# GpSimd's elementwise work moved to VectorE and ScalarE in five stages of a hybrid decoder layer

## The chip, the cores and the metric

The kernel runs on one core of a Trainium2 chip. The metric is the time of one execution on the device in microseconds. The core has TensorE (matrix products; in the profile PE, and PEld for its weight loads), VectorE (DVE), ScalarE (ACT), GpSimd (POOL) and SyncE (SP), each with a queue of its own that is worked off in order, and 16 DMA engines. Engines wait for each other by semaphores.

## The reference

One decoder layer on x of 1024 tokens by 1024 channels, in float32:

```python
h = rmsnorm(x, norm_mix)
pa, pb, pc, pg = split(h @ w_in)
ya = u * (tril(w_s) @ layernorm(v) + b_s)        # u, v = gelu(pa); chunks of 128 tokens
yb = softmax(q k^T / 8 + c_i - c_j, causal) @ v  # 8 heads of 64; c = cumsum(log_sigmoid(f))
yc = rwkv7(token_shift(pc))                      # 8 heads of 64, state per token:
     # S = S * d - (S kk) (kk a)^T + v k^T ;  y = S r ; groupnorm, bonus, gate
merged = g0 * (ya @ p_a) + g1 * (yb @ p_b) + g2 * (yc @ p_c)   # g = sigmoid(pg + bias)
x = x + merged @ w_out
x = x + (silu(gt) * up) @ w_down                 # gt, up = split(rmsnorm(x) @ w_gate_up)
return rmsnorm(x, norm_final)
```

## The kernel before

Large products are made of three matmuls each: both operands are split into a high part, cast by ScalarE to the type that TensorE takes, and a low part, the rest: `hi*hi + hi*lo + lo*hi` (L156 to L158, tiles `w_hi`, `w_lo`, `o_hi`, `o_lo`, `T_hi`, `T_lo`). The low part is one subtraction of two inputs, and who makes it is what the change is about.

The program goes through these stages, with the times of the profiled execution:

- **Head, 0 to 85 us.** x arrives in pieces, is normalised in two halves of 512 tokens (sums of squares at L470 and L473, scaling at L482 to L484), turned by TensorE (L492) and split into `h_hi` and `h_lo`. Gates are computed by a product of seven half-size products (class `Seven`, Strassen's scheme), which needs sums of blocks of h (`b11` to `b22`, `t2`) and their splits (`T1` to `T4`, `B22`, 40 operations at L335 and L336), and sums of weight blocks (`sums`, L367 to L375, splits `o_hi`, `o_lo`).
- **Gates, 85 to 345.** 14 rounds of `Seven` on `w_in` (tiles `ps_f`).
- **Recurrent branch, 345 to 885** (`rwkv_branch`). Eight units of 512 columns pass through `begin` (decay, keys `kb` and `kr`), `finish` (a triangular solve on VectorE in 31 serial steps of two operations, L1217 and L1219, tiles `tmp` and `X`) and `chain` (the state `S`). Between their steps the generator `projections` issues the other products of h (tiles `ps_g`, `ps_r`), so that TensorE has work.
- **Attention, 885 to 1200** (`attention_branch`). For each head and block of 128 queries: scores `lp` on TensorE, the gate's row `lg = cq - ck` on GpSimd (L1481) with the causal mask (L1482), the sum with row maximum on VectorE (L1485), the exponential on ScalarE (L1488), scaling (L1490), turning (L1495) and a copy to `PT` (L1496). `lg` has three buffers. Projections of v and of yc (`project`) run in between.
- **Merge and output.** 1200 to 1368: the spatial gating (`v` at L700, `ps_m`, `ya_hi`, `ya_lo`) and `project` with p_b and p_a. 1368 to 1480: `w_out` (`ps_o`). Then the second norm, the feed-forward's `Seven` (1520 to 1915) and the last product (`ps_d`), in which VectorE makes the low parts already (L947).

`w_split` (L135 to L140) splits a weight block of up to 128x1056 for all stages; its low part goes to GpSimd:

```python
nc.scalar.copy(hi, raw)
low[0].tensor_tensor(lo, raw, hi.bitcast(F32), ALU.subtract)    # low = [nc.gpsimd]
```

Weights and both parts have two buffers each. The order of instructions in each engine's queue is set by the framework's scheduler when the program is built; it follows the order of the code loosely.

Of the kernel before, what the change touches and what calls it, by code (L numbers as in the profile page):

```python
# [63 lines left out]
def kernel(ctx: ExitStack, tc: tile.TileContext, a: dict, out: bass.AP):  # L64
# [254 lines left out]
    class Seven:  # L319
# [17 lines left out]

        def prepared(self, src):
            o = [self.piece(n, (4, P), F32R) for n in ("o_hi", "o_lo")]
            self.split(o, src, nc.gpsimd)  # L340
            return o
# [14 lines left out]

        def sums(self, f, g, scratch=()):

# [9 lines left out]
            nc.vector.tensor_tensor(s2, s1, A11, ALU.subtract)  # L368
            yield self.prepared(s2)
            nc.vector.tensor_tensor(A21, A11, A21, ALU.subtract)  # L370
            yield self.prepared(A21)
            yield self.prepared(s1)
            yield self.prepared(A22)
            s4 = scratch.pop() if scratch else s2
            nc.vector.tensor_tensor(s4, A12, s2, ALU.subtract)  # L375
            yield self.prepared(s4)

# [73 lines left out]
    def low_rank(half, wts):  # L451
        for n, ci in enumerate((12, 13)):
            ps = gps.tile([P, HALF], F32, name="ps_l", tag="g")
            gemm_t(ps, wts[n], h_hi, h_lo, half)
            carry[n] = shift(ps, ci, half, carry[n], (lw, lg)[n][half])

    fetched = [gs.fetch(0)]
    load_x(1, 0)
    fetched.append(gs.fetch(1))
    load_x(1, 4)  # L460
    b11, b21, b12, b22, t2, t3 = ([None] * 4 for _ in range(6))
    for half in range(2):
        xi = x_in[half]
# [14 lines left out]
        for b in (0, 2, 1, 3):  # L478
            for q in range(4):
# [3 lines left out]
                else:  # L483
                    nc.vector.tensor_scalar(xt, xt, r[:, q:q + 1], None, op0=ALU.mult)  # L484
        if half == 0:

            ops0 = gs.sums(0, fetched[0][0], [h22_tile(i, F32).rearrange("p (a b) -> p a b", a=4) for i in range(5)])
        for k in range(4):
            for kt in (k, 4 + k):
# [5 lines left out]
                if half == 0:  # L495
                    hi, lo = hh(kt, 0)
                    nc.scalar.activation(hi, ps, AF.Copy, scale=pc("norm_mix", kt))
                    nc.vector.scalar_tensor_tensor(lo, ps, pc("norm_mix", kt), hi.bitcast(F32), op0=ALU.mult, op1=ALU.subtract)
                    nc.gpsimd.tensor_tensor(b, hi.bitcast(F32), lo.bitcast(F32), ALU.add)
                else:  # L500
                    nc.scalar.activation(b, ps, AF.Copy, scale=pc("norm_mix", kt))
            if half == 1:
                t2[k] = gs.piece("t2")
                nc.vector.tensor_tensor(b11[k], b12[k], b11[k], ALU.subtract)
                nc.vector.tensor_tensor(t2[k], b22[k], b11[k], ALU.subtract)
                nc.gpsimd.tensor_tensor(b12[k], b22[k], b12[k], ALU.subtract)
                gs.split(T2[k], t2[k], nc.vector)
        if half == 0:
            begun = [gs.begin(0, fetched[0])]
            first = [next(ops0)]  # L510
    begun.append(gs.begin(1, fetched[1]))
    for T, src in ((T3, b12), (T1, b11)):
        for k in range(4):
            gs.split(T[k], src[k], nc.vector)
            if T is T3:
                nc.gpsimd.tensor_tensor(b21[k], b21[k], t2[k], ALU.subtract)
    first += [next(ops0) for _ in range(2)]
# [34 lines left out]
    with ExitStack() as st:  # L552
# [15 lines left out]
        for half in range(2):  # L568
# [4 lines left out]
            for hp in range(4):  # L573
# [7 lines left out]
                for ps, bias, dst in ((ps_w, "c_w0", sg_d), (ps_a, "c_a0", av_d), (ps_g, None, gl_d)):  # L581
# [5 lines left out]
                    nc.sync.dma_start(dst[cs, ts], t)  # L587
    lrst.close()
    rwkv_branch(tc, a, locals())
    lora.close()  # L590


    def y_split(yd, yp, own=False):
        for k in range(4):
# [88 lines left out]
    with ExitStack() as st:  # L683
# [12 lines left out]
        for c in range(8):  # L696
# [6 lines left out]
            for half in range(2):  # L703
# [67 lines left out]
    with ExitStack() as st:  # L771
# [4 lines left out]
        for half in range(2):  # L776
# [5 lines left out]
            for b in range(4):  # L782
# [4 lines left out]
                for i in range(2):  # L787
# [216 lines left out]
def rwkv_branch(tc, a, e):  # L1004
# [4 lines left out]
    with ExitStack() as st:  # L1009
# [67 lines left out]
        def begin(n, u):  # L1077
# [58 lines left out]
        def finish(n, u):  # L1136
# [127 lines left out]
        def chain(n, u):  # L1264
# [133 lines left out]
def attention_branch(tc, a, e):  # L1398
# [6 lines left out]
    with ExitStack() as st:  # L1405
# [39 lines left out]
        for hp in range(4):  # L1445
# [10 lines left out]
            for grp in range(4):  # L1456
# [6 lines left out]
                for qi in range(2):  # L1463
# [68 lines left out]
```

## Time and profile before

| | |
|---|---|
| median of 3 runs | 2143.12 us (2140.16 to 2145.07) |
| profiled execution | 2139.3 us, span 2137.4 us |
| busy TensorE | 2000.8 us (94%), 11773 matmuls |
| busy VectorE, ScalarE, GpSimd | 1260.3, 882.2, 824.2 us |
| mean granted clock of TensorE | 0.967 |

The profile gives the busy time of each engine by stretch, groups of instructions by source line, what each engine waited for, and the instructions in order of time. The granted clock is a share of the full 2.4 GHz; 0.5 is the lower level of 1.2 GHz.

### The profile page before, as it was taken

The page shows a single profiled execution, that of the slowest core. Times are in us where ns is not written, and L with a number is a line of the kernel's source. Part 1 is how long each engine was busy: PE and PEld are TensorE (multiplying, and loading weights), DVE is VectorE, ACT ScalarE, POOL GpSimd, SP SyncE. Part 2 cuts the span into 40 slices and gives each one's busy share as a digit, 9 for nine tenths or more (in the row PEclk, how much of TensorE's full clock was granted, in tenths as well). Part 3 has the DMA queues.
Part 4 walks back from the last instruction along what each step waited for, and adds up shares of the span by engine and source line. Part 5 has one row for each costly group of instructions (what it writes and reads, how often), then busy time and mean ns, then how long its engine had stood idle before and what let it go on. Part 6 is the DMA issues. An engine that isn't in the chain of part 4 may idle for free. (4 is left out here: it accounts for less than half of the span.)

```text
span 2137.4 us, 31459 instructions
## 1 busy us (share of the span) xinstructions
PE 2000.8 (94%) x11773; PEld 1598.6 (75%) x11773; DVE 1260.3 (59%) x2398; ACT 882.2 (41%) x1566; POOL 824.2 (39%) x630
## 2 busy tenths in 40 slices
PE   5899999899889899899999989998999999999998
PEld 4688886676777667777666668897778887878886
DVE  8754454777677764245466594436655444556966
ACT  6433335334454454357554322245323222224435
POOL 5654451223232232233444432344676666530000
PEclk8899999899999999999899999999999999999999
DMA  4233335333233322543343753443232332349433
GB/s 124 84 112 116 116 102 195 108 92 107 83 111 93 94 81 80 171 116 99 104 125 102 274 180 99 129 154 98 79 111 90 115 99 91 107 158 327 135 99 123
DMA packets 254700, 260.91 MB, mean 122 GB/s; under 512 B 21430, under 2 KB 195588, under 8 KB 254548
## 3 DMA queue, kind: packets, MB, share of 16 engines
q1 hardware_dynamic: 218388, 208.53, 31.1%
q10 hardware_dynamic: 32928, 41.16, 6.0%
q0 software_dynamic: 3232, 9.21, 1.6%
q8 instruction: 92, 1.51, 0.3%
q14 instruction: 60, 0.49, 0.1%
HBM read 176.77 MB, written 77.89 MB: 119 GB/s over the span
## 5 line engine op out<-in xcount | busy, mean ns | idle before, releaser
L139 POOL TENSOR_TENSOR w_lo<-w_raw,w_hi 128x1024 fp32r<-128x1024 f32 (+2 forms) x114 | 271.1, 2380 | 438.9 <-ACT w_hi L138 438.6
L156 PE MATMUL ps_f<-T_hi,o_hi 128*128 128x512 f32 x576 | 226.7, 394 | 8.4 <-ACT o_hi L335 5.9
L157 PE MATMUL ps_f<-T_lo,o_hi 128*128 128x512 f32 x576 | 227.2, 394 | 7.4 <-DVE T_lo L336 7.4
L158 PE MATMUL ps_f<-T_hi,o_lo 128*128 128x512 f32 x576 | 226.1, 393 | 0.4 <-POOL o_lo L336 0.4
L336 POOL TENSOR_TENSOR o_lo<-s,o_hi 128x512 fp32r<-128x512 f32 x105 | 150.8, 1436 | 85.1 <-ACT o_hi L335 79.1
L138 ACT CAST w_hi<-w_raw 128x1024 fp32r<-128x1024 f32 (+2 forms) x114 | 112.6, 989 | 138.2 <-PE ps_p L157 30.0
L156 PEld LDWEIGHTS ps_f<-T_hi,o_hi 128*128 128x128 f32 x576 | 109.1, 189 | 34.2 <-ACT o_hi L335 6.3
L157 PEld LDWEIGHTS ps_f<-T_lo,o_hi 128*128 128x128 f32 x576 | 109.2, 190 | 32.5 <-DVE T_lo L336 9.4
L158 PEld LDWEIGHTS ps_f<-T_hi,o_lo 128*128 128x128 f32 x576 | 109.3, 190 | 24.0 <-POOL o_lo L336 0.8
L157 PE MATMUL ps_d<-w_lo,a_hi 128*128 128x512 f32 x272 | 106.7, 392 | 1.7 <-DVE w_lo L947 1.7
L158 PE MATMUL ps_d<-w_hi,a_lo 128*128 128x512 f32 x272 | 106.7, 392 | 0.0
L156 PE MATMUL ps_d<-w_hi,a_hi 128*128 128x512 f32 x272 | 104.7, 392 | 0.0
L335 ACT CAST o_hi<-s 128x512 fp32r<-128x512 f32 x105 | 65.0, 619 | 94.2 <-DVE s L368 45.8
L367 DVE TENSOR_TENSOR s<-up_raw 128x512 f32<-128x512 f32 x35 | 27.9, 797 | 126.1 <-DMA up_raw<-in_w_gate_up_dram 118.2
L336 POOL TENSOR_TENSOR o_lo<-up_raw,o_hi 128x512 fp32r<-128x512 f32 x70 | 90.5, 1293 | 27.0 <-ACT o_hi L335 15.6
L375 DVE TENSOR_TENSOR s<-w_raw,s 128x512 f32<-128x512 f32 x35 | 60.3, 1724 | 59.9 <-POOL o_lo L336 59.9
L1481 POOL TENSOR_SCALAR lg<-ck,cq 128x128 f32<-128x128 f32 (+7 forms) x64 | 50.4, 788 | 100.9 <-PE tp L1495 95.5
L871 ACT CAST a_hi<-a_raw 128x1024 fp32r<-128x1024 f32 (+1 forms) x42 | 41.2, 981 | 110.9 <-PE ps_d L157 92.3
L1217 DVE TENSOR_TENSOR tmp<-N,X 128x60 f32<-128x60 f32 (+24 forms) x248 | 77.1, 311 | 9.3 <-DMA N<-nd 1.5
L156 PE MATMUL ps_g<-h_hi,w_hi 128*128 128x512 f32 x192 | 81.6, 425 | 1.0 <-ACT w_hi L138 1.0
L1485 DVE CUSTOM_DVE_ANT_0 lg<-lp,lg 128x128 f32<-128x128 f32 (+7 forms) x64 | 47.9, 753 | 56.2 <-POOL lg L1482 48.6
L158 PE MATMUL ps_g<-h_hi,w_lo 128*128 128x512 f32 x192 | 76.9, 400 | 2.0 <-POOL w_lo L139 2.0
(485 smaller groups left out, 5760.7 us busy)
## 6 DMA issues: line engine op xcount, KB each, us to landing
w_raw<-in_w_in_dram SPq DMA_DIRECT2D x50, 512.0 KB, 4.2
gt<-gate_d ACTq DMA_DIRECT2D x24, 512.0 KB, 3.4
up_raw<-in_w_gate_up_dram SPq DMA_DIRECT2D x44, 256.0 KB, 3.2
w_raw<-in_w_gate_up_dram SPq DMA_DIRECT2D x22, 512.0 KB, 3.9
a_raw<-act_S SPq DMA_DIRECT2D x20, 512.0 KB, 4.1
w<-in_w_down_dram SPq DMA_DIRECT2D x18, 512.0 KB, 6.3
gate_d<-c SPq DMA_DIRECT2D x33, 256.0 KB, 2.1
w_raw<-in_w_out_dram SPq DMA_DIRECT2D x16, 512.0 KB, 5.7
```

The lines of the kernel that those rows point to most:

```text
L138: nc.scalar.copy(hi, raw)
L139: low[0].tensor_tensor(lo, raw, hi.bitcast(F32), ALU.subtract)
L156: nc.tensor.matmul(ps, lhs[0], rhs[0], start=first, stop=False)
L157: nc.tensor.matmul(ps, lhs[0], rhs[1], start=False, stop=False)
L158: nc.tensor.matmul(ps, lhs[1], rhs[0], start=False, stop=last)
L335: nc.scalar.copy(dst[0], src)
L336: eng.tensor_tensor(dst[1], src, dst[0].bitcast(F32), ALU.subtract)
L375: nc.vector.tensor_tensor(s4, A12, s2, ALU.subtract)
L871: nc.scalar.copy(hi, raw)
L1217: nc.vector.tensor_tensor(tv, N[:, 0:kx, kx].unsqueeze(1).to_broadcast([P, m, kx]), X[:, i0:8, kx:kx + 1].to_broadcast([P, m, kx]), ALU.mult)
L1481: nc.gpsimd.tensor_scalar(lg[:, 0:nk], ck[h][:, 0:nk], -1.0, cq[:, qb, hd:hd + 1], op0=ALU.mult, op1=ALU.add)
L1485: nc.vector.tensor_tensor_reduce(lg[:, 0:nk], lp[:, 0:nk], lg[:, 0:nk], 1.0, NEG, ALU.add, ALU.max, mx)
```

## The change

The elementwise work of GpSimd goes to VectorE in the head (first two weight blocks, five `o_lo`, `b12`, `b21`), in the recurrent branch (`w_lo`, half of `kb`, `x_lo`, `y_lo`), in the attention and the projections (`w_lo`, `y_lo`, `ya_lo`) and in w_out (`w_lo`). In the head the copies `b` of the first half are made by ScalarE from PSUM, deferred by four tiles, and the normalisation of the second half is written ahead of the first gate's products. The gate's rows of the attention go to ScalarE. In the rounds of `Seven` for gates and feed-forward GpSimd keeps its work: `low[0]` is switched over and back.

```diff
-        def prepared(self, src):
+        def prepared(self, src, eng=None):
             o = [self.piece(n, (4, P), F32R) for n in ("o_hi", "o_lo")]
-            self.split(o, src, nc.gpsimd)
+            self.split(o, src, eng or nc.gpsimd)
...
+    low[0] = nc.vector
     fetched = [gs.fetch(0)]
     load_x(1, 0)
     fetched.append(gs.fetch(1))
     load_x(1, 4)
+    low[0] = nc.gpsimd
...
-    for half in range(2):
+    def normed(half):
...
+    def turned(half, xi):
+        plain = []
...
-                    nc.gpsimd.tensor_tensor(b, hi.bitcast(F32), lo.bitcast(F32), ALU.add)
+
+                    plain.append((b, ps, kt))
+                    for b_, ps_, kt_ in [plain.pop(0)] if len(plain) > 4 else []:
+                        nc.scalar.activation(b_, ps_, AF.Copy, scale=pc("norm_mix", kt_))
...
-                nc.gpsimd.tensor_tensor(b12[k], b22[k], b12[k], ALU.subtract)
+                nc.vector.tensor_tensor(b12[k], b22[k], b12[k], ALU.subtract)
...
-        if half == 0:
-            begun = [gs.begin(0, fetched[0])]
-            first = [next(ops0)]
+    xi0, _ = normed(0)
+    turned(0, xi0)
+    xi1, root = normed(1)
+
+    ops0 = gs.sums(0, fetched[0][0], [h22_tile(i, F32).rearrange("p (a b) -> p a b", a=4) for i in range(5)], nc.vector)
+    begun = [gs.begin(0, fetched[0])]
+    first = [next(ops0)]
+    turned(1, xi1)
     begun.append(gs.begin(1, fetched[1]))
...
-                nc.gpsimd.tensor_tensor(b21[k], b21[k], t2[k], ALU.subtract)
+                nc.vector.tensor_tensor(b21[k], b21[k], t2[k], ALU.subtract)
...
     lrst.close()
+    low[0] = nc.vector
     rwkv_branch(tc, a, locals())
...
-            nc.gpsimd.tensor_tensor(lo, raw, hi.bitcast(F32), ALU.subtract)
+            nc.vector.tensor_tensor(lo, raw, hi.bitcast(F32), ALU.subtract)
...
-                nc.gpsimd.tensor_tensor(lo[:, sl], uf, hi[:, sl].bitcast(F32), ALU.subtract)
+                nc.vector.tensor_tensor(lo[:, sl], uf, hi[:, sl].bitcast(F32), ALU.subtract)
...
             if half == 1:
+                low[0] = nc.gpsimd
                 fs = Seven(fx, 25, (B11, B21) + (None,) * 5, w_gu, lambda f: (f * P, DFF + f * P), act_done)
...
-            nc.gpsimd.tensor_tensor(hl[1], sq, hl[0].bitcast(F32), ALU.subtract)
+            nc.vector.tensor_tensor(hl[1], sq, hl[0].bitcast(F32), ALU.subtract)
...
-                nc.gpsimd.tensor_tensor(kb[hs, :, 1 - h, :], v3(av)[hs], v3(pi)[hs], ALU.mult)
+                nc.vector.tensor_tensor(kb[hs, :, 1 - h, :], v3(av)[hs], v3(pi)[hs], ALU.mult)
...
-            nc.gpsimd.tensor_tensor(hl[1], r, hl[0].bitcast(F32), ALU.subtract)
+            nc.vector.tensor_tensor(hl[1], r, hl[0].bitcast(F32), ALU.subtract)
...
-                        nc.gpsimd.tensor_scalar(lg[:, 0:nk], ck[h][:, 0:nk], -1.0, cq[:, qb, hd:hd + 1], op0=ALU.mult, op1=ALU.add)
+                        nc.scalar.activation(lg[:, 0:nk], ck[h][:, 0:nk], AF.Identity, bias=cq[:, qb, hd:hd + 1], scale=-1.0)
```

VectorE at the end of the head, before (`T..` and `h22` are low parts of h's sums, `u` the first round's result):

```order
L336 TENSOR_TENSOR T42_lo_199<-b_335,T42_hi_198 128x512
L336 TENSOR_TENSOR T43_lo_201<-b_353,T43_hi_200 128x512
L336 TENSOR_TENSOR h22_609<-b_480,h22_608 128x512
L336 TENSOR_TENSOR h22_613<-b_500,h22_612 128x512
L336 TENSOR_TENSOR h22_617<-b_520,h22_616 128x512
L336 TENSOR_TENSOR h22_605<-b_460,h22_604 128x512
L382 TENSOR_TENSOR u_357<-u_357,ps_f_626 128x512
```

The same place now (`o_lo` are low parts of the weight sums):

```order
L336 TENSOR_TENSOR o_lo_580<-h22_409,o_hi_579 128x512
L336 TENSOR_TENSOR T40_lo_195<-b_293,T40_hi_194 128x512
L336 TENSOR_TENSOR o_lo_584<-h22_407,o_hi_583 128x512
L336 TENSOR_TENSOR T41_lo_197<-b_309,T41_hi_196 128x512
L336 TENSOR_TENSOR T42_lo_199<-b_326,T42_hi_198 128x512
L336 TENSOR_TENSOR T43_lo_201<-b_344,T43_hi_200 128x512
L336 TENSOR_TENSOR o_lo_596<-h22_408,o_hi_595 128x512
L336 TENSOR_TENSOR h22_613<-b_500,h22_612 128x512
L336 TENSOR_TENSOR o_lo_601<-h22_405,o_hi_600 128x512
L336 TENSOR_TENSOR h22_609<-b_480,h22_608 128x512
L336 TENSOR_TENSOR h22_617<-b_520,h22_616 128x512
L336 TENSOR_TENSOR h22_605<-b_460,h22_604 128x512
```

The four later `o_lo`, which stood in GpSimd's queue, now stand between the splits of VectorE.

VectorE in a triangular solve of the recurrent branch, before:

```order
L1217 TENSOR_TENSOR tmp_3748<-N_3742,X_3747 128x66
L1219 TENSOR_TENSOR X_3747<-X_3747,tmp_3748 128x6x11
L1217 TENSOR_TENSOR tmp_3748<-N_3742,X_3747 128x60
L1219 TENSOR_TENSOR X_3747<-X_3747,tmp_3748 128x6x10
L1217 TENSOR_TENSOR tmp_3748<-N_3742,X_3747 128x54
L1219 TENSOR_TENSOR X_3747<-X_3747,tmp_3748 128x6x9
L1217 TENSOR_TENSOR tmp_3748<-N_3742,X_3747 128x48
```

The same steps now:

```order
L1234 TENSOR_TENSOR tmp_3748<-N_3742,X_3747 128x66
L1236 TENSOR_TENSOR X_3747<-X_3747,tmp_3748 128x6x11
L1234 TENSOR_TENSOR tmp_3748<-N_3742,X_3747 128x60
L1236 TENSOR_TENSOR X_3747<-X_3747,tmp_3748 128x6x10
L139 TENSOR_TENSOR w_lo_3994<-w_raw_3991,w_hi_3993 128x1024
L445 SCALAR_TENSOR_TENSOR gt_3975<-ps_g_3920,omu_140,sh_3976 128x512
L1234 TENSOR_TENSOR tmp_3748<-N_3742,X_3747 128x54
L441 MEMSET sh_4075 128x1
L1236 TENSOR_TENSOR X_3747<-X_3747,tmp_3748 128x6x9
```

A weight split of 128x1024 stands between two steps of the solve; there are 29 of them in the branch. 36 of the 114 `w_lo` stay on GpSimd.

ScalarE in the attention, first group of queries, before (L1488 is the exponential, L1496 the copy of the turned rows):

```order
L1488 ACTIVATE lg_8755,sm_8763<-lg_8755,mx_8760 128x256
L1496 COPY PT_8696<-tp_8730 128x128
L1488 ACTIVATE lg_8787,sm_8795<-lg_8787,mx_8792 128x384
L1496 COPY PT_8695<-tp_8751 128x2x128
L284 ACT_TABLE_LOAD
L284 ACTIVATE gt_8883<-ps_r_8882 128x256
L1496 COPY PT_8696<-tp_8767 128x2x128
L1488 ACT_TABLE_LOAD
L1488 ACTIVATE lg_8804,sm_8812<-lg_8804,mx_8809 128x384
L1496 COPY PT_8779<-tp_8799 128x3x128
```

The same place now (L1505 and L1513 are those two, L1498 the gate's row):

```order
L1505 ACTIVATE lg_8739,sm_8747<-lg_8739,mx_8744 128x256
L1498 ACTIVATE lg_8755<-ck_8451,cq_72 128x256
L1513 COPY PT_8696<-tp_8730 128x128
L1498 ACTIVATE lg_8787<-ck_8449,cq_72 128x384
L1513 COPY PT_8695<-tp_8751 128x2x128
L1498 ACTIVATE lg_8804<-ck_8451,cq_72 128x384
L1505 ACTIVATE lg_8755,sm_8763<-lg_8755,mx_8760 128x256
L1505 ACTIVATE lg_8787,sm_8795<-lg_8787,mx_8792 128x384
L284 ACT_TABLE_LOAD
L284 ACTIVATE gt_8883<-ps_r_8882 128x256
L1513 COPY PT_8696<-tp_8767 128x2x128
```

Gate rows for later blocks stand between exponentials and copies. ScalarE's queue now holds 77 table loads, where it held 71.

## Rows read from the trace of the kernel before

**Rows 1.** busy time of each engine by stretch: PE, PEld, DVE, ACT, POOL, clock, DMA

```profile
0.00:85.00 85.00, 53.61 (x208) 40.29 (x209) 71.28 (x120) 49.11 (x104) 50.46 (x41) 0.86 0.37 109
85.00:345.00 260.00, 259.62 (x1129) 211.62 (x1128) 137.46 (x186) 97.11 (x151) 128.25 (x88) 1.00 0.36 106
345.00:885.00 540.00, 491.69 (x4365) 378.06 (x4364) 343.04 (x902) 250.49 (x489) 146.95 (x107) 0.95 0.34 104
885.00:1200.00 315.00, 296.71 (x1767) 221.31 (x1766) 159.91 (x435) 170.04 (x317) 124.19 (x171) 0.93 0.43 130
1200.00:1280.00 80.00, 68.03 (x322) 54.16 (x321) 67.58 (x111) 18.95 (x28) 37.52 (x27) 0.96 0.74 240
```

**Rows 2.** what TensorE waited for: us in total, times, longest

```profile
PE ps_m L710 <- DVE v L700: 9.9, 15, 1.7
PE ps_r L157 <- POOL w_lo L139: 9.9, 6, 3.6
...
PE ps_f L157 <- DVE T_lo L336: 7.4, 4, 3.1
```

**Rows 3.** timeline of VectorE and GpSimd in the head: start, us, operation

```profile
9.67 0.43 DVE L470 CUSTOM_DVE_ANT_0 junk_v<-x_in 128x256 f32<-128x256 f32 x1 [0.29 <-DMA x_in<-in_x_dram]
...
58.55 6.78 POOL L336 TENSOR_TENSOR o_lo<-h,o_hi 128x512 fp32r<-128x512 f32 x4 [0.61 <-POOL b L516]
...
59.02 11.45 DVE L336 TENSOR_TENSOR T_lo<-b,T_hi 128x512 fp32r<-128x512 f32 x8
70.40 2.48 DVE L336 TENSOR_TENSOR h<-b,h 128x512 fp32r<-128x512 f32 x4
```

**Rows 4.** groups by line and shape, VectorE, 0 to 85 us: busy us, mean ns

```profile
L336 DVE TENSOR_TENSOR T_lo<-b,T_hi 128x512 fp32r<-128x512 f32 x12 | 15.2, 1315 | 0.0
L470 DVE CUSTOM_DVE_ANT_0 junk_v<-x_in 128x256 f32<-128x256 f32 x16 | 14.0, 873 | 6.8 <-DMA x_in<-in_x_dram 6.7
```

**Rows 5.** timeline of VectorE and GpSimd in the triangular solve

```profile
586.44 0.27 DVE L1217 TENSOR_TENSOR tmp<-N,X 128x60 f32<-128x60 f32 x1
...
586.93 5.06 POOL L139 TENSOR_TENSOR w_lo<-w_raw,w_hi 128x1056 fp32r<-128x1056 f32 x2 [11.34 <-ACT w_hi L138]
...
587.00 2.43 DVE L1217 TENSOR_TENSOR tmp<-N,X 128x54 f32<-128x54 f32 x1
```

**Rows 6.** groups by line, GpSimd, 345 to 885 us

```profile
L139 POOL TENSOR_TENSOR w_lo<-w_raw,w_hi 128x1024 fp32r<-128x1024 f32 (+1 forms) x29 | 69.7, 2406 | 167.7 <-ACT w_hi L138 167.5
L1123 POOL TENSOR_TENSOR kb<-av,pi 64x512 f32<-64x512 f32 x16 | 26.2, 1636 | 89.9 <-DVE av L1117 89.3
```

**Rows 7.** groups by line, the whole execution

```profile
L1217 DVE TENSOR_TENSOR tmp<-N,X 128x60 f32<-128x60 f32 (+24 forms) x248 | 77.1, 311 | 9.3 <-DMA N<-nd 1.5
...
L157 PE MATMUL ps_o<-w_lo,m_hi 128*128 128x256 f32 x256 | 72.4, 283 | 3.8 <-POOL w_lo L139 3.8
...
L1481 POOL TENSOR_SCALAR lg<-ck,cq 128x128 f32<-128x128 f32 (+7 forms) x64 | 50.4, 788 | 100.9 <-PE tp L1495 95.5 <-DVE sm L1489 2.0 <-DVE mx L1486 1.2
...
L1488 ACT ACTIVATE lg<-lg,mx 128x128 f32<-128x128 f32 (+7 forms) x64 | 49.5, 774 | 21.4 <-DVE mx L1486 18.9 <-DVE sm L1489 1.5 <-POOL lg L1482 0.8
...
L947 DVE TENSOR_TENSOR w_lo<-w,w_hi 128x1024 fp32r<-128x1024 f32 x30 | 36.6, 1221 | 8.0 <-ACT w_hi L946 7.8
```

**Rows 8.** all waits: us in total, times, longest

```profile
POOL lg L1481 <- PE tp L1495: 95.5, 44, 8.2
...
DVE lg L1485 <- POOL lg L1482: 48.6, 36, 4.6
```

**Rows 9.** timeline of ScalarE around a table load in the attention

```profile
926.18 1.28 ACT L1488 ACT_TABLE_LOAD   x1 [0.36 <-DVE mx L1486]
927.48 0.51 ACT L1488 ACTIVATE lg<-lg,mx 128x256 f32<-128x256 f32 x1
```

**Rows 10.** groups by line and shape, VectorE, 1200 to 1280 us

```profile
L616 DVE TENSOR_TENSOR macc<-macc,gt 128x512 f32<-128x512 f32 x15 | 16.1, 1076 | 0.1
```

More of the change, by code (lines that the diff above doesn't have):

```diff
@@ L355, in begin, with sums @@
             return g, u, c11
-        def sums(self, f, g, scratch=()):
+        def sums(self, f, g, scratch=(), eng=None):
             c = self.cols(f)[1]
@@ L368, in sums @@
             nc.vector.tensor_tensor(s2, s1, A11, ALU.subtract)
-            yield self.prepared(s2)
+            yield self.prepared(s2, eng)
             nc.vector.tensor_tensor(A21, A11, A21, ALU.subtract)
-            yield self.prepared(A21)
-            yield self.prepared(s1)
-            yield self.prepared(A22)
+            yield self.prepared(A21, eng)
+            yield self.prepared(s1, eng)
+            yield self.prepared(A22, eng)
             s4 = scratch.pop() if scratch else s2
             nc.vector.tensor_tensor(s4, A12, s2, ALU.subtract)
-            yield self.prepared(s4)
+            yield self.prepared(s4, eng)
         def rest(self, f, begun, ops, fps):
@@ L484 @@
                     nc.vector.tensor_scalar(xt, xt, r[:, q:q + 1], None, op0=ALU.mult)
-        if half == 0:
-            ops0 = gs.sums(0, fetched[0][0], [h22_tile(i, F32).rearrange("p (a b) -> p a b", a=4) for i in range(5)])
+        return xi, root
+    def turned(half, xi):
+        plain = []
         for k in range(4):
@@ L505 @@
                 nc.vector.tensor_tensor(t2[k], b22[k], b11[k], ALU.subtract)
-                nc.gpsimd.tensor_tensor(b12[k], b22[k], b12[k], ALU.subtract)
+                nc.vector.tensor_tensor(b12[k], b22[k], b12[k], ALU.subtract)
                 gs.split(T2[k], t2[k], nc.vector)
-        if half == 0:
-            begun = [gs.begin(0, fetched[0])]
-            first = [next(ops0)]
+        for b_, ps_, kt_ in plain:
+            nc.scalar.activation(b_, ps_, AF.Copy, scale=pc("norm_mix", kt_))
+    xi0, _ = normed(0)
[5 more added lines that the diff above has]
+    turned(1, xi1)
     begun.append(gs.begin(1, fetched[1]))
@@ L1329, in chain @@
             nc.scalar.activation(hl[0], y, AF.Square)
-            nc.gpsimd.tensor_tensor(hl[1], sq, hl[0].bitcast(F32), ALU.subtract)
+            nc.vector.tensor_tensor(hl[1], sq, hl[0].bitcast(F32), ALU.subtract)
             yield
```

## Prediction

> **What bounds the kernel now.** I read the busy times by stretch first, to find where TensorE is the limit and where it isn't [rows 1]. In 85 to 345 us it is busy for 259.6 of 260 us at granted clock 1.00. GpSimd is busy 128 us there, and no split that GpSimd makes there can be worth anything while that holds. The change leaves GpSimd its work in that stretch and in the feed-forward. What can move is elsewhere: up to 85 us TensorE is busy 53.6 us at clock 0.86, in the recurrent branch (345 to 885) 491.7 of 540 at 0.95, in the attention (885 to 1200) 296.7 of 315 at 0.93, in the merge after it 68.0 of 80 at 0.96. Idle TensorE time in these four adds up to 31.4 + 48.3 + 18.3 + 12.0 = 110 us. Then I read what TensorE waited for [rows 2]: 9.9 us for VectorE's normalised v in the merge, 9.9 us in six waits for GpSimd's w_lo, 7.4 us in four waits for VectorE's T_lo in the head. The groups by line add 3.8 us for w_lo in w_out [rows 7]. Last the timeline, for why VectorE was late [rows 3, 5].
>
> **What a VectorE operation loses beside GpSimd.** In the head eight T_lo subtractions take 11.45 us from 59.02 (1.43 each) while GpSimd runs its o_lo at 58.55 and w_lo after it; the four of the same shape at 70.40, when GpSimd has stopped, take 2.48 us, 0.62 each [rows 3]. In the triangular solve an operation of 0.27 us takes 2.43 us when it starts just behind a w_lo of GpSimd [rows 5]. So a small operation on VectorE waits out a whole large one of GpSimd. The change removes such pairs in the stages that are not bound by TensorE. Each moved operation is also cheaper: two w_lo of GpSimd take 5.06 us [rows 5], VectorE's own w_lo of 128x1024 takes 1.22 each [rows 7].
>
> **Head.** VectorE is the bound: 71.3 of 85 us busy [rows 1], and TensorE waits for its T_lo. Removed: the excess over the undisturbed price, 12 x (1.315 - 0.68) = 7.6 us in T_lo<-b and 16 x (0.873 - 0.43) = 7.1 us in the sums of squares, whose undisturbed instances take 0.43 [rows 4, 3]; other groups have it too, so 14.7 is a floor. Added to VectorE: two w_lo, 2.4 us, and five o_lo, four b12 and four b21 at 0.62 to 0.68, 8 to 9 us: 11 us. The eight b go to ScalarE, 49.1 of 85 us busy, at some 0.7 each (an estimate from its 0.774 for the rows of the attention, whose mean width is a little larger [rows 7]): 5.5 us more, in its gaps. By the two rows alone VectorE gains 4 us; with T_lo<-t, the differences and the first sums of the weights, all of the same shape, it is about 12. I walked the new order of VectorE at 0.61 us per 128x512 operation, with ScalarE's casts where they come later: its last h22 ends some 10 us earlier than the 72.9 us of before [rows 3]. The normalisation of the second half now stands ahead of TensorE's first products of the gate, but TensorE idles there already. I take 10 us (4 to 13). Nothing behind it can eat that, since the next stretch is TensorE at its limit from the start.
>
> **Waits for w_lo.** 9.9 + 3.8 = 13.7 us over eight waits, at most 3.6 us each. Where two blocks are split in succession, as at 586.93, two splits end 2.6 us sooner on VectorE (5.06 - 2.44). VectorE's queue is in order, however, and the split stands in it between solve steps and state updates; whatever waits there for ScalarE's w_hi holds all behind it. I take 10 of the 13.7 (bounds +10, if it is late by as much as it is early now, and -13.7).
>
> **Recurrent branch, otherwise.** GpSimd gives up 29 w_lo (69.7 us) and 16 kb (26.2 us) [rows 6] and 24 splits of 128x512. On VectorE they cost 29 x 1.22 + 16 x 0.68 + 24 x 0.68 = 62.6 us. Given back: in the solve's first operation 248 x (0.311 - 0.27) = 10 us [rows 7, 5], and more in its second one and in the kb products, which run beside GpSimd as well. VectorE goes from 343 us to at most 396 of 540, so it is not the bound, and the chain loses 1 us and more at each kb (1.64 on GpSimd, 0.68 on VectorE). Against that stands the blocking of the queue. I take -4 us (bounds -21 and +20), since most of the waits that remain are hops between TensorE and ScalarE, which the change does not touch.
>
> **Attention.** The 64 rows of the forget gate take 50.4 us on GpSimd; the exponentials over the same shapes take 49.5 us on ScalarE [rows 7], so I price the moved rows at that. ScalarE is busy 170 of 315 us [rows 1], with them 220: room, but the work is on the path of the softmax. On GpSimd 95.5 us were spent waiting for TensorE's transposes, which set the buffer free, and nobody stood behind; VectorE waited 48.6 us for the mask behind those rows [rows 8]. On ScalarE the exponentials and the copies of P stand behind that wait. In favour: w_lo and y_lo no longer get between a gate row and its mask on GpSimd, and VectorE's scaling is not held up. I take 0 (bounds -12 and +32).
>
> ScalarE reloads its table in this stretch; the next activation starts 1.30 us after a load starts [rows 9], and the new order has 77 loads where there were 71: 7.8 us, in its idle time. The Trainium skill, page ScalarE: Activation LUTs, section What ACT_TABLE_LOAD costs, puts a drain behind each load and some 2.66 us in all; that would be 16 us, and the row here speaks against it.
>
> The Trainium skill's GPSIMD Engine Reference, section Engine selection, speaks against this part of the change: GpSimd is twice as slow only with two inputs, and about at line rate with one. The gate row has one input, and the two rows above (788 and 774 ns) agree with it. By that rule the move saves nothing in itself and only loads the busier engine, which is the third rival.
>
> **Merge.** VectorE is the bound there (67.6 of 80 us). Added: 16 ya_lo, 8 w_lo of 128x512 and about three of 128x1024: 24 x 0.62 + 3 x 1.22 = 18.5 us. Given back: 15 x (1.076 - 0.68) = 5.9 us in macc [rows 10], and some in v and u. Between 0 and +12.6; I take +4.
>
> **Sum.** -10 - 10 - 4 + 0 + 4 = -20. Idle TensorE also lowers its clock: in the recurrent branch 540 x (1 - 0.95) = 27 us of full-rate time beside 48 us of idleness [rows 1], 0.56 per us. I count a quarter for the 20 us: -5. Together -25. The profiled execution took 2139.3 us, so 2114; the median of the runs shown is 2143.1, 3.8 us above it, so I predict 2118.
>
> **Rivals.**
> 1. All that is late beside GpSimd goes: head -13, all w_lo waits -14, VectorE's other waits in the recurrent branch -13, the attention -6, and the clock gives back 0.2 to 0.3 of it. -55, so 2088. For it: the long operations of [rows 5] sit in the serial solve. Against: that stage is TensorE-bound by nine tenths.
> 2. VectorE's queue gives back what the locks cost. w_lo, x_lo and y_lo wait in order for ScalarE; a GpSimd that idles costs nothing, a VectorE that idles holds up the solve and the state. Of 29 splits in the branch each would have to stop it for half a microsecond on the path: +15 there, -10 in the head, and the rest even: -5, so 2138. Against: the solve's single steps are short and have slack of a third of the time.
> 3. Slower: ScalarE becomes the bound of the attention. If a third of the 95.5 us that GpSimd waited for transposes now stands on ScalarE in front of exponentials and copies, and TensorE has no other work there, it costs 32 us. With -25 elsewhere that is +7: 2150. It decides from 25 us on, a quarter of that wait. For it: the clock there is already 0.93, so TensorE has pauses that it could lengthen. Against: TensorE is 94% busy over the stretch, with projections to fill in between.
> That the change does not do what it says is excluded by the order: 36 w_lo stay on GpSimd of 114, in the stretches that TensorE bounds and at their ends.
>
> **Chances.** Forecast (-13 to -40) 0.50, with 2103 to 2130 as its own range; first rival 0.20; second (-13 to +4) 0.17; third 0.13. What a measurement tells from no change is 0.2%, 4.3 us. Half of the second rival is under that bound: faster 0.50 + 0.20 + 0.09 = 0.79; same 0.07; slower 0.14. The range holds 8 in 10 from 2088, the first rival's middle, to 2150, the third's.
>
> **What would show it.** Right: T_lo of 0.62 to 0.68 us throughout the head and TensorE busy without a gap from some 65 us on; in the solve no operation over 0.5 us; TensorE's waits for w_lo below 4 us; the stretches of gates and feed-forward as long as before. Wrong: VectorE waiting long for ScalarE's w_hi in the recurrent branch, TensorE waiting for P or for the row maximum in the attention at clock 0.5, or a merge of over 85 us.

## The result and the profile after

The changed kernel takes 2105.05 us (median of 4 runs, 2104.27 to 2108.1); the kernel before took 2141.64 us beside it. The ratio is 0.9832, with a 95% interval of 0.9812 to 0.9852: faster by 36 us (32 to 40). Predicted were 25 us, with a range of its own of 13 to 40.

The busy times by stretch (columns as in [rows 1]). The first stretch ends at the same time as there, 85 us; the later ones are cut at about the same places in the program, and 842 to 1160 us answers to 885 to 1200:

```profile
0.00:85.00 85.00, 63.79 (x262) 49.81 (x263) 66.27 (x143) 57.16 (x117) 19.10 (x22) 0.92 0.37 112
85.00:330.00 245.00, 243.14 (x1057) 197.92 (x1057) 128.76 (x176) 91.45 (x142) 120.10 (x83) 1.00 0.37 111
330.00:842.00 512.00, 488.57 (x4389) 377.72 (x4388) 347.44 (x975) 252.49 (x493) 29.57 (x38) 0.97 0.36 110
842.00:867.00 25.00, 21.12 (x174) 20.51 (x172) 9.52 (x15) 11.24 (x18) 3.72 (x8) 1.00 1.00 294
867.00:1160.00 293.00, 272.89 (x1584) 198.14 (x1583) 162.22 (x439) 207.08 (x370) 29.18 (x77) 0.92 0.38 113
1160.00:1240.00 80.00, 66.55 (x315) 54.26 (x314) 69.85 (x136) 19.42 (x28) 0.00 (x0) 0.89 0.70 233
```

Against [rows 1] TensorE has 10 us more work inside the first 85 us, and the branch has shrunk from 540 to 512 us. VectorE is busy there for 347 us where it was 343, although it took over the work of [rows 6] and more: its own operations became shorter by nearly as much as was added. From the branch's end to the merge (842 to 1160 us) ScalarE is busy 218 us, 48 more than in [rows 1], and the clock of the attention is no higher than before.

Starts of TensorE's products, in us, say where the time went (`ps_l` ends the gates, `ps_g` begins and `ps_var` ends the branch, `ps_m` begins the merge, `ps_o` w_out):

| profiled run | first ps_l | first ps_g | last ps_var | first ps_m of the merge | first ps_o | span |
|---|---|---|---|---|---|---|
| before | 322.6 | 364.3 | 885.7 | 1200.5 | 1368.8 | 2137.4 |
| after | 310.4 | 350.1 | 841.6 | 1161.8 | 1333.1 | 2102.6 |
| head_only | 310.1 | 353.6 | 875.8 | 1196.3 | 1363.5 | 2135.3 |
| branch_only | 321.3 | 362.9 | 856.1 | 1176.2 | 1342.6 | 2113.0 |
| late_back | 308.7 | 348.3 | 843.8 | 1173.9 | 1344.6 | 2114.0 |
| lg_pool | 309.6 | 349.1 | 840.9 | 1158.9 | 1326.8 | 2096.3 |
| lg_pool_v_scalar | 309.8 | 349.6 | 842.2 | 1156.9 | 1323.5 | 2092.1 |
| after_v_scalar | 307.7 | 346.7 | 838.7 | 1153.3 | 1319.5 | 2090.7 |

By the marks the head gave 12.2 us (to `ps_l`), the stretch to `ps_g` another 2.0, the branch 29.9 (521.4 to 491.5), the attention cost 5.4 (314.8 to 320.2), merge and projections 3.0 (168.3 to 171.3), and w_out and the rest cost 0.9.

VectorE in the head by line and shape, answering to [rows 4]:

```profile
L336 DVE TENSOR_TENSOR T_lo<-b,T_hi 128x512 fp32r<-128x512 f32 x12 | 7.8, 685 | 0.0
L472 DVE CUSTOM_DVE_ANT_0 junk_v<-x_in 128x256 f32<-128x256 f32 x16 | 6.8, 422 | 6.7 <-DMA x_in<-in_x_dram 6.6
```

1315 ns became 685, and 873 became 422. The timeline of VectorE where `o_lo` and `T_lo` now alternate (start, us, operation) has no stretched operation left:

```profile
54.15 2.49 DVE L336 TENSOR_TENSOR T_lo<-b,T_hi 128x512 fp32r<-128x512 f32 x4
56.56 0.69 DVE L336 TENSOR_TENSOR o_lo<-h,o_hi 128x512 fp32r<-128x512 f32 x1
57.16 0.69 DVE L336 TENSOR_TENSOR T_lo<-b,T_hi 128x512 fp32r<-128x512 f32 x1
```

The groups of the whole execution that answer to [rows 7]:

```profile
L139 DVE TENSOR_TENSOR w_lo<-w_raw,w_hi 128x1024 fp32r<-128x1024 f32 (+2 forms) x78 | 86.7, 1112 | 51.2 <-ACT w_hi L138 49.3 <-PE ps_a L594 1.7
...
L157 PE MATMUL ps_o<-w_lo,m_hi 128*128 128x256 f32 x256 | 73.3, 286 | 2.5 <-DVE w_lo L139 2.5
...
L1234 DVE TENSOR_TENSOR tmp<-N,X 128x60 f32<-128x60 f32 (+24 forms) x248 | 60.4, 244 | 7.6 <-DMA N<-nd 0.3
...
L1236 DVE TENSOR_TENSOR X<-X,tmp 128x60 f32<-128x60 f32 (+24 forms) x248 | 52.4, 211 | 7.5
```

Both operations of the solve are faster, 311 to 244 ns and 275 to 211; the second line of before was

```profile
L1219 DVE TENSOR_TENSOR X<-X,tmp 128x60 f32<-128x60 f32 (+24 forms) x248 | 68.3, 275 | 8.1
```

The first line of after shows the feared stop, too: VectorE stood 49 us for ScalarE's `w_hi` with a split at the head of its queue, 22 us of them in the branch.

What TensorE waited for in the whole run, answering to [rows 2]:

```profile
PE ps_p L158 <- DVE w_lo L139: 10.5, 4, 2.6
...
PE ps_r L157 <- DVE w_lo L139: 4.2, 2, 3.1
...
PE ps_o L157 <- DVE w_lo L139: 2.5, 1, 2.5
```

The large waits for v in the merge and for T_lo are gone. In place of the wait for v TensorE waits 10.5 us in the projection of the merge, for a `w_lo` that stands behind VectorE's own work there.

In the branch TensorE's waits fell from 45.7 to 22.8 us. By the engine waited for: GpSimd 8.0 us before, all of it for `w_lo`, and none after; VectorE 21.0 and then 10.3, with 3.5 for `w_lo` in the latter; ScalarE 16.7 and 12.4. The four largest of the waits for GpSimd and VectorE, before:

```profile
PE ps_r L157 <- POOL w_lo L139: 5.9, 3, 3.6
PE zp L1289 <- DVE S L1310: 5.6, 7, 2.1
PE ps_s L1151 <- DVE kr L1127: 4.4, 1, 4.4
PE ps_r L156 <- DVE z L289: 3.5, 3, 2.6
```

After (the one for `z` is gone):

```profile
PE ps_r L157 <- DVE w_lo L139: 3.1, 1, 3.1
PE ps_s L1168 <- DVE kr L1144: 2.9, 1, 2.9
PE zp L1306 <- DVE S L1327: 0.6, 1, 0.6
```

### The profile page after: what moved, and what is told of

Read it like the earlier page. It is cut to its first block, busy times and chain, and to the rows that moved or that the text cites. A ratio compares the mean times of both kernels' runs of the same rounds, so it can differ in the third digit from the quotient of the medians.

```text
span 2102.6 us, 31344 instructions
## 1 busy us (share of the span) xinstructions
PE 1992.8 (95%) x11773; PEld 1596.1 (76%) x11773; DVE 1280.4 (61%) x2553; ACT 936.7 (45%) x1644; POOL 474.4 (23%) x403
## 4 chain that ended last, share of the span: by engine, by line
PE 63%; DVE 11%; issue 9%; ACT 8%; POOL 5%; DMA 3%; SPq 0%; ACTq 0%; POOLq 0%; DVEq 0%
PE ps_f L158 6%; PE ps_f L156 6%; PE ps_f L157 6%; PE ps_d L157 3%; PE ps_d L158 3%; PE ps_d L156 3%; PE ps_g L156 3%; POOL o_lo L336 3%; PE ps_g L158 3%; PE ps_g L157 3%; PE ps_p L158 3%; PE ps_p L156 3%; PE ps_p L157 2%; PE op L1518 2%; POOL c L763 2%
## 5 line engine op out<-in xcount | busy, mean ns | idle before, releaser
L156 PEld LDWEIGHTS ps_f<-T_hi,o_hi 128*128 128x128 f32 x576 | 109.2, 190 | 34.3 <-ACT o_hi L335 10.3
L139 POOL TENSOR_TENSOR w_lo<-w_raw,w_hi 128x1024 fp32r<-128x1024 f32 x36 | 91.3, 2537 | 126.8 <-ACT w_hi L138 87.1
L139 DVE TENSOR_TENSOR w_lo<-w_raw,w_hi 128x1024 fp32r<-128x1024 f32 (+2 forms) x78 | 86.7, 1112 | 51.2 <-ACT w_hi L138 49.3
L335 ACT CAST o_hi<-up_raw 128x512 fp32r<-128x512 f32 x70 | 43.1, 615 | 80.9 <-POOL o_lo L336 77.8
L156 PE MATMUL ps_f<-B_hi,w_hi 128*128 128x512 f32 x176 | 71.5, 406 | 7.4 <-ACT u L353 7.4
```

The lines of the kernel that those rows point to most:

```text
L156: nc.tensor.matmul(ps, lhs[0], rhs[0], start=first, stop=False)
L335: nc.scalar.copy(dst[0], src)
```

## The experiments

Ratios are to the kernel before, run beside it on the same chip.

**The head alone, and the branch alone.** Edits of `head_only`: all of the diff ahead of `lrst.close()`, nothing behind it. Of `branch_only`, to the kernel before:

```diff
+    low[0] = nc.vector
     rwkv_branch(tc, a, locals())
+    low[0] = nc.gpsimd
...
-            nc.gpsimd.tensor_tensor(hl[1], ...            # x_lo, y_lo, three places
+            nc.vector.tensor_tensor(hl[1], ...
-                nc.gpsimd.tensor_tensor(kb[hs, :, 1 - h, :], ...
+                nc.vector.tensor_tensor(kb[hs, :, 1 - h, :], ...
```

> The kernel before with the head of the changed kernel alone (two w_lo, five o_lo, b12, b21 on VectorE, b on ScalarE, the normalisation of the second half ahead of the first products). Theory, the stages add up: 10 to 14 us faster than before, since the first product of low_rank came 12.2 us earlier in the changed kernel (322.6 to 310.4 us) and TensorE has no slack from there to the branch; ratio about 0.9944. Rival, the branch takes it back, because it was the branch's own waits that the earlier start lengthens: under 5 us, ratio above 0.9975.

> The kernel before with w_lo, kb, x_lo and y_lo of the recurrent branch alone on VectorE. Theory: 26 to 34 us faster than before (ratio 0.984 to 0.988), all of it between the first ps_g (364.3 us before) and the last ps_var (885.7 us before). Rival: the 30 us between these two marks in the changed kernel came in part from how the branch met the head's earlier end and the order that the scheduler made of both; then the branch alone gives under 20 us.

Measured: 0.9954 (0.9936 to 0.9972), 10 us, and 0.9855 (0.9833 to 0.9877), 31 us. The stages are worth about the same alone as together. Which of the head's edits gave its 10 us (the moved subtractions, `b` on ScalarE or the earlier normalisation) was not tried. The branch's stretch from `ps_g` to `ps_var` went from 522 us to 493. Before:

```profile
364.00:886.00 522.00, 476.10 (x4297) 369.95 (x4296) 335.10 (x883) 239.10 (x472) 143.72 (x101) 0.95 0.32 98
```

The branch alone:

```profile
363.00:856.00 493.00, 468.32 (x4294) 365.51 (x4293) 334.25 (x949) 239.46 (x472) 32.94 (x35) 0.97 0.35 104
```

VectorE (third busy time) does 66 operations more in 0.9 us less. TensorE's idle time fell by 21 us (522 - 476.1 against 493 - 468.3), and the clock rose from 0.95 to 0.97, which took 8 us off the busy time of the same products. Both kernels show a longer attention than before (320.5 and 320.1 us from `ps_var` to `ps_m`, before 314.8), though neither changes anything there; so a stretch of that length can come out 5 us longer with no edit in it. What TensorE idles in it differs less, as the part on the gate's rows shows.

**The branch in parts.** `branch_wlo`, `branch_kb` and `branch_hl` each make one of the three edits of `branch_only`.

> The kernel before with only the w_lo of the recurrent branch on VectorE; kb, x_lo and y_lo stay on GpSimd. Theory (stretched VectorE work): GpSimd's long operations are gone from the solve, 16 to 26 us faster than before, ratio 0.988 to 0.9925; VectorE's means of tmp and X fall to 250 and 215 ns. Rival (kb, x_lo and y_lo are links of the chain that leads to each unit's first product, and they gave most): under 12 us.

> The kernel before with only the 16 kb products of GpSimd on VectorE; w_lo, x_lo and y_lo stay on GpSimd. Theory: 3 to 8 us faster (ratio 0.996 to 0.9985), since VectorE's own 16 kb fall from 1.18 to 0.70 us and kr is no longer late, 4.4 us of wait. Rival (kb is a link of the chain): 12 us or more, ratio below 0.9945.

> The kernel before with only x_lo and y_lo of the recurrent branch (24 splits of 128x512) on VectorE; w_lo and kb stay on GpSimd. Theory (stretched VectorE work): 30.8 us of GpSimd's 127 us of two-input work in the branch go, so some 3 to 10 us of gain, ratio 0.995 to 0.9985, and the three parts together (27.7 for w_lo, 13.9 for kb, this one) are more than the 31 us of all three. Rival: VectorE's queue is held by ScalarE's x_hi and y_hi, ratio 1.000 or more.

Measured: 0.9871 (0.9845 to 0.9896) for w_lo, 0.9935 (0.9911 to 0.996) for kb, 0.9984 (0.9969 to 1.0) for x_lo and y_lo. w_lo alone gives 28 of the 31 us, and 5 operations of the solve over 0.5 us remain of 20. kb alone gives 14, more than the 3 to 8 expected; the rival's 12 or more came out, though the interval reaches down to 9. Its gain doesn't come from the solve, where 19 such operations remain, 36 us together (before 37). Together with x_lo and y_lo it adds only 3 us to what w_lo gives, so the gains overlap. In kb's profile TensorE's idle time in the branch fell by only 4 us (45.9 to 41.6), the rest is clock; why kb alone gives so much stays open. x_lo and y_lo are at the edge of what can be told from nothing.

**Stretched work, or earlier splits?** `branch_twin` is `branch_only`, and GpSimd computes each of the branch's w_lo a second time, into a tile that nobody reads:

```diff
...
         low[0].tensor_tensor(lo, raw, hi.bitcast(F32), ALU.subtract)
+        if twin:
...
+            nc.gpsimd.tensor_tensor(again, raw, hi.bitcast(F32), ALU.subtract)
...
```

> The kernel with only the recurrent branch's splits and kb on VectorE, and besides GpSimd makes each of the branch's 29 w_lo once more into a scratch tile that nobody reads. Theory (what the branch gained is VectorE's work that is no longer stretched while GpSimd works): VectorE's solve operations are stretched again (mean of tmp from 244 ns to about 290, of X from 211 to about 250) and 12 to 25 us of the 31 us are lost: ratio to before 0.991 to 0.997. Rival (what the branch gained is that w_lo and kb are made sooner and cheaper by VectorE): the twin delays nobody, ratio within 0.003 of 0.9855.

Measured: 1.0067 (1.0041 to 1.0093). The twin takes away the whole gain and 14 us more, 45 us in all, where the theory expected 12 to 25; the kernel has GpSimd's operations beside VectorE and the splits in VectorE's queue as well. The solve's means are 319 and 228 ns, the first above and the second below what was expected. The timeline of its solve, VectorE and GpSimd (`issue`: the profile shows nothing that GpSimd waited for):

```profile
587.95 0.27 DVE L1225 TENSOR_TENSOR tmp<-N,X 128x66 f32<-128x66 f32 x1
588.26 0.23 DVE L1227 TENSOR_TENSOR X<-X,tmp 128x66 f32<-128x66 f32 x1
588.43 2.43 POOL L143 TENSOR_TENSOR again<-w_raw,w_hi 128x1056 bf16<-128x1056 f32 x1 [13.79 <-issue]
588.52 2.43 DVE L1225 TENSOR_TENSOR tmp<-N,X 128x60 f32<-128x60 f32 x1
590.98 0.22 DVE L1227 TENSOR_TENSOR X<-X,tmp 128x60 f32<-128x60 f32 x1
```

It is the picture of [rows 5] again: an operation of 0.27 us that starts 0.09 us behind GpSimd's ends 0.09 us behind it. In the changed kernel no operation of the solve is longer than 0.5 us. Before there were 20, of 37 us together: each of them begins inside a subtraction of GpSimd (14 in a w_lo, 6 in an x_lo), and none of the other 476 does.

`branch_twin_one` puts two copies of `w_hi`, operations of one input, in the place of the twin's subtraction:

```diff
-            nc.gpsimd.tensor_tensor(again, raw, hi.bitcast(F32), ALU.subtract)
+            for _ in range(2):
+                nc.gpsimd.tensor_copy(again, hi.bitcast(F32))
```

> As the kernel with the twin, but GpSimd copies w_hi twice into the scratch tile, an operation of one input, in place of the subtraction of two inputs; it waits for the same cast of ScalarE and is about as long. Theory A (only GpSimd's operations of two inputs stretch VectorE's): the means of tmp and X stay at 244 and 211 ns, and the time is that of the branch without twin, ratio 0.983 to 0.990. Theory B (any work of GpSimd stretches VectorE's, or the twin lost 42 us by holding buffers and by the new order): ratio above 0.998.

Measured: 1.0005 (0.9989 to 1.0022). Theory A fell, by the time and by the solve's means, 285 and 255 ns. Its solve:

```profile
583.50 2.19 POOL L144 CAST again<-w_hi 128x1056 bf16<-128x1056 f32 x2 [13.80 <-ACT w_hi L138]
583.63 1.00 DVE L1226 TENSOR_TENSOR tmp<-N,X 128x60 f32<-128x60 f32 x1
584.67 1.09 DVE L1228 TENSOR_TENSOR X<-X,tmp 128x60 f32<-128x60 f32 x1
585.79 0.25 DVE L1226 TENSOR_TENSOR tmp<-N,X 128x54 f32<-128x54 f32 x1
```

The two copies hold two operations of VectorE for a copy's length each. That GpSimd's operation has a single input doesn't help. The Trainium skill, page SBUF — State Buffer, section Who interferes with whom, says that VectorE and GpSimd share a pair of ports under an exclusive lock, and that a VectorE operation with two inputs in SBUF contends for it with a GpSimd operation that reads SBUF. These two timelines agree, with 2.43 us for 0.27 and 1.00 for 0.27.

What the twins don't separate: they also hold the weights' buffers a little longer, and the queues are in another order. The longer hold can be no more than a part: of the 27 us by which TensorE's waits in the branch are longer in the first twin than in `branch_only` (51.7 and 24.6 us), 6 are for low parts of weights (11.2 and 4.8). The largest part is for the state, 15.0 us in eight waits, 0.6 without the twin:

```profile
PE zp L1297 <- DVE S L1318: 15.0, 8, 4.8
```

**The gate's rows.** `lg_pool` is the changed kernel with L1498 as it was before; `late_back` is the changed kernel with all splits behind the branch back on GpSimd and the rows left on ScalarE:

```diff
     rwkv_branch(tc, a, locals())
+    low[0] = nc.gpsimd
...
-            nc.vector.tensor_tensor(lo, raw, hi.bitcast(F32), ALU.subtract)           # y_lo
+            nc.gpsimd.tensor_tensor(lo, raw, hi.bitcast(F32), ALU.subtract)
-                nc.vector.tensor_tensor(lo[:, sl], uf, hi[:, sl].bitcast(F32), ALU.subtract)   # ya_lo
+                nc.gpsimd.tensor_tensor(lo[:, sl], uf, hi[:, sl].bitcast(F32), ALU.subtract)
```

> The changed kernel with the gate's rows of the attention back on GpSimd (64 of them). Theory, ScalarE lengthens the attention: the stretch from the first lp to the last tp falls from 287.5 us by 10 to 15 us, and the time goes to 2090 to 2095 us (ratio to before 0.976 to 0.978). Rival, the attention grew because w_lo and y_lo stand in VectorE's queue or because of the instructions' new order: the time stays within 4 us of the changed kernel's 2105 us; if GpSimd's rows also stretch VectorE's work again, it is slower than that.

> The changed kernel with all splits behind the recurrent branch back on GpSimd (w_lo, y_lo and ya_lo in the attention, the projections and w_out), the gate's rows still on ScalarE. Theory (ScalarE's rows are what the attention lost): attention as long as in the changed kernel, 283 to 292 us from first lp to last tp, merge 1 to 4 us shorter, w_out up to 4 us longer by its waits for w_lo, the sum within 5 us of 2105 us. Rival (VectorE's splits are what the attention lost): attention 10 us or more shorter, 2095 us or less.

Measured: 0.9789 (0.977 to 0.9808) and 0.9877 (0.9856 to 0.9898). With the rows back on GpSimd the kernel is 9 us faster than the changed one by the ratios, less than expected. The stretch from the first lp to the last tp fell as expected, from 287.5 to 275.9 us, but the marks moved by only 2.2 us in the attention, and by 3.4 behind it. `late_back` met neither expectation: the attention grew by 10 us more, to 330.1 us. The waits for the gate's rows in the attention show what changed. The changed kernel:

```profile
POOL lg L1499 <- ACT lg L1498: 175.9, 48, 14.0
...
DVE sm L1506 <- ACT lg L1505: 26.6, 27, 2.5
...
DVE lg L1502 <- POOL lg L1499: 21.1, 29, 2.6
```

With the rows on GpSimd:

```profile
DVE lg L1502 <- POOL lg L1499: 46.1, 37, 3.6
...
DVE sm L1506 <- ACT lg L1505: 9.6, 12, 2.1
```

With splits on GpSimd and rows on ScalarE:

```profile
DVE sm L1507 <- ACT lg L1506: 41.1, 31, 2.6
...
DVE lg L1503 <- POOL lg L1500: 25.6, 32, 2.3
```

VectorE's wait goes from the masked row to the exponential: on ScalarE the rows stand between the exponentials. When GpSimd has the splits besides, the mask (L1499), which now comes after ScalarE's row, queues behind a `w_lo`; that this is the cause of the 10 us was read from the queues, not tried. TensorE's waits for the row maximum behind that mask are 1.5 us in the changed kernel and 7.6 in `late_back`.

TensorE's idle time in the attention says more than its length. Before, after, and with the rows back on GpSimd, from the last `ps_var` to `ps_m` (second and third number: length and busy TensorE):

```profile
885.70:1200.50 314.80, 296.51 (x1764) 221.21 (x1764) 159.91 (x435) 170.04 (x317) 124.09 (x170) 0.93 0.43 130
```

```profile
841.60:1161.80 320.20, 296.22 (x1765) 220.49 (x1764) 171.74 (x454) 219.76 (x388) 32.90 (x85) 0.93 0.43 127
```

```profile
840.90:1158.90 318.00, 300.73 (x1765) 223.11 (x1764) 174.06 (x455) 173.61 (x322) 89.34 (x149) 0.92 0.44 129
```

That is 18.3, 24.0 and 17.3 us of idleness, and TensorE's waits for ScalarE are 8.2, 16.7 and 9.4 us of it. The eight kernels with the attention of before idle 18.0 to 19.7 us in it; the extra length of `head_only` and `branch_only` (19.5 and 19.2 us of idleness) is clock. In the two kernels of the next part, with the rows on ScalarE and on GpSimd, it idles 20.6 and 18.4 us, with 15.9 and 9.6 of it for ScalarE. So the rows on ScalarE cost TensorE 2 to 7 us of waiting there; the rest of the differences in length shows as a lower clock.

**The merge.** VectorE has 64 operations of 0.34 us there that ScalarE could do. `lg_pool_v_scalar` adds this to `lg_pool`, `after_v_scalar` to the changed kernel:

```diff
-                nc.vector.tensor_scalar(v[:, t, :], v[:, t, :], mv[:, t, 0:1], rs[:, t:t + 1], op0=ALU.subtract, op1=ALU.mult)
+                nc.scalar.activation(v[:, t, :], v[:, t, :], AF.Identity, bias=nm[:, t:t + 1], scale=rs[:, t:t + 1])
...
+        nm = sb.tile([P, NT], F32, name="nm")
+        nc.vector.scalar_tensor_tensor(nm, mv[:, :, 0], -1.0, rs, op0=ALU.mult, op1=ALU.mult)
```

> The changed kernel with the gate's rows on GpSimd, and v in the merge normalised by ScalarE (64 activations with scale and bias by token, in place of 64 operations of VectorE of 0.34 us). Theory (VectorE's order holds w_lo back in the merge; TensorE waits 12.5 us for it there): 21 us of VectorE's 74 go to ScalarE, which is busy 19 of 80 us; 5 to 10 us faster than 2098 us, ratio 0.974 to 0.9765. Rival (transfers bound the merge, 0.74 of the DMA engines' time, or ScalarE's casts w_hi and ya_hi then stand behind v): no faster than the 0.9789 of the kernel with the rows on GpSimd.

> The changed kernel, its gate's rows left on ScalarE, with v in the merge normalised by ScalarE. Theory (VectorE's order is what the merge is short of): the stretch from the first ps_m to the first ps_o falls from 171.3 us to about 166, as it fell from 167.9 to 166.6 us with the rows on GpSimd, and 3 to 8 us of time go: ratio 0.9795 to 0.982. Rival (the 0.9753 of the kernel with both edits owes its distance from 0.9789 to the spread between measurements): ratio 0.983 to 0.985.

Measured: 0.9753 (0.973 to 0.9777) and 0.9776 (0.9746 to 0.9806), 8 and 12 us better than the same kernel without it; the 8 us are at the edge, since the intervals overlap a little. On ScalarE such an operation takes 481 ns where VectorE's took 344, and TensorE's waits for `w_lo` in the merge went from 12.5 to 2.3 us with the rows on GpSimd, from 10.5 to 2.5 in the changed kernel. With the rows on GpSimd:

```profile
L718 ACT ACTIVATE v<-v,nm,rs 128x128 f32<-128x128 f32 x48 | 19.2, 481 | 12.9 <-DMA v<-v_d 12.9
```

```profile
PE ps_p L158 <- DVE w_lo L139: 2.3, 4, 1.1
```

From `ps_m` to `ps_o` this gave 5.1 us in the changed kernel and 1.3 with the rows on GpSimd; the remainder lies ahead of it, in the attention for the most part, where the first of these operations already stand; its cause isn't shown. With v on ScalarE the place of the gate's rows can't be told any more, the two intervals overlap. So the cost of the rows on ScalarE in the whole time lies between nothing and 9 us.

**Four buffers for the rows.** `best_lg4` is `lg_pool_v_scalar` with `bufs=4` for `lg`:

```diff
-                        lg = sb.tile([P, S], F32, name="lg", tag="lg", bufs=3)
+                        lg = sb.tile([P, S], F32, name="lg", tag="lg", bufs=4)
```

> The kernel with the gate's rows on GpSimd and v on ScalarE, with four lg buffers in place of three. Theory (the rows on GpSimd wait for the transposes that free a buffer, and VectorE waits 46 us for the masked rows): VectorE's wait for them falls below 25 us and the time by 3 to 8 us, ratio 0.9715 to 0.974. Rival (VectorE is not late for TensorE in the attention; TensorE's pauses there are hops between engines): within 0.002 of 0.9753.

Measured: 0.9793 (0.9765 to 0.9822), no gain, if anything a loss. VectorE's wait for the masked rows fell from 43.0 to 32.5 us, not below the 25 expected, and TensorE's clock in the stretch was lower:

```profile
842.00:1162.00 320.00, 303.84 (x1761) 223.32 (x1761) 170.69 (x440) 174.32 (x334) 89.90 (x149) 0.91 0.43 128
```

against three buffers:

```profile
842.00:1157.00 315.00, 296.64 (x1765) 219.79 (x1765) 170.89 (x440) 179.62 (x338) 89.14 (x149) 0.93 0.44 130
```

VectorE isn't the one who is late there. TensorE idles 16 us in the first and 18 in the second; the 5 us between them are clock, not waiting. In the merge, which the edit doesn't touch, the four buffers' profile is another 6 us longer (172.8 and 166.6 us from `ps_m` to `ps_o`). The best kernel is `lg_pool_v_scalar`, 0.9753, faster than the kernel before and the changed one; from `after_v_scalar` (0.9776) it can't be told apart.

## Why the prediction was right, point by point

The direction and the size came out: 36 us where 25 were forecast, within its own range but near its end (2105 us, from 2103 on). The mechanism was right, and the total is in part luck: one term was too small by some 14 us, and others came out worse than forecast and took part of that back.

- **Head, -10:** right. 12.2 us by the marks, 10 us alone; TensorE idles 10 us less up to `ps_l` (31.4 and 21.2 us). T_lo takes 685 ns, VectorE's last h22 ends at 63.9 us where it was 72.9, and TensorE's last pause of over 0.4 us ends at 57.3 us, where before one ended at 72.9.
- **Waits for w_lo, -10:** somewhat too large. At the places named it gave 7 us (9.9 to 4.2 us in `ps_r`, 3.8 to 2.5 in `ps_o`). Over the whole run TensorE waits as long for w_lo as before, because of the 10.5 us in `ps_p`; but those stand where the 9.9 us for v stood (now 0.5), and belong to the merge.
- **Recurrent branch otherwise, -4:** the term that was mis-sized. The branch gave 29.9 us. Its waits for w_lo account for 4.5 and the clock for 7 (time at the lower level in the stretch, halved: 23.9 us before, 17.1 after), so some 18 are this term's. The step that failed is the reason given for the 4 us, that most of the waits that remain are hops between TensorE and ScalarE, which the change does not touch. Of the 37.7 us of waits other than for w_lo, 21.0 were for VectorE, and 14 of them went; of the 16.7 for ScalarE another 4 went. The undisturbed price was off as well: it was taken from one step of the solve, 0.27 us, where the group's means without GpSimd are 244 and 211 ns. With those the first operation gives back 17 us, not 10, and the second, which the sum left without a price, 16. The blocking of VectorE's queue, set against it, is real, and was named as a sign of being wrong: VectorE stood 22 us for `w_hi` in the branch. But TensorE waited only 3.5 us there for a split of VectorE.
- **Attention, 0:** it came out 5.4 us longer, within the bounds. TensorE idled 5.7 us more, and its waits for ScalarE rose by 8.5 us: the third rival's mechanism, at about a fifth of its 32 us. What the other moves gave there didn't make up for it.
- **Merge, +4:** 3.0 us by the marks, half of it idleness of TensorE (12.0 and 13.5 us, now all behind VectorE), half clock (0.98 and 0.94). With the same merge `lg_pool` took 167.9 us, as long as before, so a cost of that size isn't shown.
- **Clock, -5:** right in sum. Time at the lower level fell from 141.9 to 130.8 us over the run, which is 5.5 us at half rate. By stretch, halved, it fell by 5 us in the head, 2 from there to `ps_g` and 7 in the branch, and rose by 2 in the attention and 7 in the merge; the prediction's reason, less idleness, fits the head and the branch.
- **The rivals:** the first named the right cause (what is late beside GpSimd goes) and 13 us for VectorE's other waits in the branch, where 14 went; it erred in the attention and the merge, where TensorE's idleness grew. The second needed half a microsecond on the path for each of 29 splits, which those 3.5 us are far from.

## What to carry to other kernels

Take the undisturbed price of an operation from the whole group, by comparing instances that run beside a GpSimd operation with those that don't, and sum the difference over the stage: from `ps_g` to `ps_var` VectorE was busy 335 us before, with GpSimd's help, and 336 us after, without it. Then ask of each wait of TensorE which engine it is for, before calling it out of reach. In this kernel's serial chain of short VectorE operations with two inputs in SBUF, a GpSimd operation that read SBUF beside it cost the chain up to its own length, and VectorE's queue, which had gaps, did the same work for less. Where VectorE is the bound, as in the merge here, work with one tensor input can go to ScalarE if that has room: 481 ns there were cheaper for the kernel than 344 on VectorE.

## What was not expected of the hardware

- A copy with one input on GpSimd holds VectorE's two-input operations just as a subtraction does: 0.27 us became 1.00 us, and 0.23 us 1.09 us, behind copies of about 1.1 us each.
- VectorE's operation on one PSUM and one SBUF operand (`A<-ps_s,mask`) isn't held: in the kernel before, twelve of them begin inside a two-input operation of GpSimd and take 680 to 694 ns, and the mean in the changed kernel, without GpSimd beside them, is 687.
- The same attention took from 314.0 us (`branch_kb`) to 327.0 us (`branch_twin_one`) in kernels that leave it alone, with 18 and 19 us of idle TensorE and a granted clock of 0.94 and 0.90. A change of a few us in its length can't be read from one profile; its idle time varied by less than 2 us.
